# Stick-breaking attention: two-head score tiles in two PSUM banks, the second sigmoid in SBUF, units in a written order

## The chip, the cores and the metric

The kernel runs on one core of one Trainium2 chip. The metric is the device time of one execution in microseconds (us). Five engines work side by side, each through its own queue in order: TensorE (PE in the profile; PEld are its weight loads), VectorE (DVE), ScalarE (ACT), GpSimd (POOL) and SyncE (SP), which issues most DMAs.

## The reference

Two transformer layers on a sequence of 2048 tokens, width 1024. The first layer has six heads of stick-breaking attention, six of differential attention and four of memory attention; the second has sliding-window and memory attention. The change is in the six stick-breaking heads (head size 64), whose reference is, for a block of 128 queries:

```python
z = jnp.einsum('bqhd,bkhd->bhqk', qi, k, preferred_element_type=jnp.float32) * scale
strict = key_idx[None, :] < q_idx[:, None]
log_1mb = jnp.where(strict, jax.nn.log_sigmoid(-z), 0.0)
rc = jnp.flip(jnp.cumsum(jnp.flip(log_1mb, axis=-1), axis=-1), axis=-1)
after = rc - log_1mb
w = jnp.where(strict, jnp.exp(jax.nn.log_sigmoid(z) + after), 0.0)
return jnp.einsum('bhqk,bkhd->bqhd', w.astype(v.dtype), v)
```

So the weight of a key is sigmoid(z) times the product of sigmoid(-z) over all keys between it and the query. The kernel forms that product with a scan from the last key to the first.

## The kernel before

One launch runs stages one after the other: layer-1 projections, gates, stick-breaking, differential attention, the output product with layer norm, then layer 2. A scheduler that works with modelled times orders the instructions on each engine; where code goes through `PinnedCore`, the named engines keep the order in which the code is written (such instructions carry the helper's line, L55, in the profile, and L57 in the changed file).

Stick-breaking (`stick_breaking`) works on three pairs of heads (p), four blocks of 512 queries (t, from the last), four blocks of 128 queries in each (qi, from the last), and chunks of 512 keys (c, from the diagonal backwards). One (p, t, qi, c) is called a unit here; there are 120. A unit on the diagonal has 512, 384, 256 or 128 columns (qi = 3 to 0), every other 512. For each of a unit's two heads the steps are:

- scores: two matmuls (L572) into a PSUM bank z, and on the diagonal a third that adds the mask (L575);
- ScalarE: sigmoid(z/8) into an SBUF tile wb (L577), then sigmoid(-z/8) over z in PSUM (L578);
- VectorE: a scan (L581) of running products from PSUM into an SBUF row of products; its second operand is a column of zeros in SBUF; GpSimd sets each row's last element to 1 (L563);
- wb times that row (L585), four times in five on GpSimd and once on VectorE;
- `tblocks`: up to four TensorE transposes into a bank tp (L474), copied to SBUF as wT in turn by ScalarE (L121) and VectorE (L123);
- values (L591): per block of 128 keys one product for each head, into halves of the bank pv. Each stands in the trace as two records.

At the end of a block t VectorE multiplies pv by a gate (L595), and SyncE stores it. PSUM has four banks for z, three for tp, one for pv. None of the stage's instructions go through `PinnedCore`. When p = 2 and t = 1 are reached in the code, `filler` asks for the first weights of the next stage's background work: loads into rx, CASTs on ScalarE into wo (L871), subtractions on GpSimd (L872). The scheduler is free to put these earlier.

Of the kernel before, what the change touches and what calls it, by code (L numbers as in the profile page):

```python
# [7 lines left out]
F32 = mybir.dt.float32  # L8
# [3 lines left out]
AF = mybir.ActivationFunctionType  # L12
ALU = mybir.AluOpType
# [4 lines left out]
P = 128  # L18
NB = S // P
TC = 512  # L20
NT = S // TC
# [11 lines left out]
FT = 1  # L33
# [5 lines left out]
FILL = 0.95  # L39
PRODUCTS = ((), (0, 1), (), (2, 3))  # L40
# [24 lines left out]
class Net:  # L65
# [216 lines left out]
    def layer1_proj(self):  # L282
        nc, dr = self.nc, self.dr
# [82 lines left out]
        for k, _ in enumerate(gates):  # L366
            if k == 24 + GATES_A:
                self.sb_first = self.load_sb(0)
# [158 lines left out]
    def load_sb(self, p):  # L527

        qs = self.load_qstack(self.sbq[p], NT - 1)
# [8 lines left out]
        return ks, vp, qs  # L538

    def stick_breaking(self):  # L540
        nc = self.nc
        for p in range(3):
            ks, vp, qs = self.load_sb(p) if p else self.sb_first
            for t in range(NT - 1, -1, -1):
                if p == 2 and t == FT:
                    self.fill = self.filler()
                    for f in next(self.fill):
                        f()
                    self.dk, self.dq = {}, {}
                    self.load_dq(0, 0, 0)  # L550
                    for c in range(NT - 1):
                        self.load_dk(0, c)
                if t < NT - 1:
                    qs = self.load_qstack(self.sbq[p], t)
                sl = self.load_silu(self.silu[p], t)
                pv = self.psum("pv")
                for qi in range(3, -1, -1):
                    qb = 4 * t + qi
                    qcol = slice(qi * P, (qi + 1) * P)
                    n = (qb + 1) * P  # L560
                    pr = [self.t("row") for _ in range(2)]
                    for hh in range(2):
                        nc.gpsimd.memset(pr[hh][:, n - 1:n], 1.0)  # L563
                    for c in range(qb // 4, -1, -1):
                        lo, hi = c * 512, min(n, c * 512 + 512)
                        m = hi - lo
                        ws = []
                        for hh in range(2):
                            z = self.psum("z")
                            diag = hi == n  # L570
                            for k in range(2):
                                nc.tensor.matmul(z[:, :m], qs[:, hh, k, qcol], ks[hh][:, lo:hi], start=(k == 0),  # L572
                                                 stop=(k == 1 and not diag))
                            if diag:
                                nc.tensor.matmul(z[:, m - P:m], self.identb, self.mask[:, 2 * P + 1:3 * P + 1], start=False, stop=True)  # L575
# [12 lines left out]
                        for j in range(m // P):  # L588
                            blk = c * 4 + j
                            for hh in range(2):  # L590
                                nc.tensor.matmul(pv[64 * hh:64 * hh + 64, qcol], vp[:, blk, 64 * hh:64 * hh + 64],  # L591
                                                 wT[hh][:, j * P:(j + 1) * P],
                                                 start=(hi == n and j == 0), stop=(c == 0 and j == m // P - 1))
                mt = self.t("c2")
                nc.vector.tensor_mul(mt, pv, sl)  # L595
                self.dma(self.m1[p, :, t * TC:(t + 1) * TC], mt, nc.scalar if p == 2 and t == 0 else None)

# [765 lines left out]
    def run(self):  # L1363
        nc, dr, i = self.nc, self.dr, self.i
        with self.phase({"kv": 6, "qs": 2}, {}):
# [4 lines left out]
            with self.phase({"row": 5, "wb": 5, "wT": 5, "c2": 2, "sl": 2}, {"z": 4, "tp": 3, "pv": 1}, "right"):  # L1370
                self.stick_breaking()
# [95 lines left out]
```

## Time and profile before

| | |
|---|---|
| median of 3 runs | 2593.26 us (2591.59 to 2594.64) |
| profiled execution, its own time | 2590.89 us |
| its span, first to last instruction | 2589.1 us |
| mean granted TensorE clock | 0.983 of full speed |
| TensorE, VectorE, ScalarE, GpSimd busy in the span | 95%, 63%, 49%, 35% |
| stick-breaking stage in the span | about 720 to 1117 us |

The span is measured inside one execution; its own time also holds what lies around it. The stage's limits are read from the first score matmul at 720.63 us and the last multiplication by a gate, which begins at 1117.24 us.

### The profile page before, as it was taken

The numbers are of one execution on the slowest core, as the hardware profiler recorded it, in microseconds if no ns is written. First come the engines' busy times: TensorE is split into PE (matmuls) and PEld (weight loads), VectorE is DVE, ScalarE is ACT, GpSimd is POOL, SyncE is SP. The second block draws the span as 40 slices with busy tenths as digits, with TensorE's granted clock in tenths as the row PEclk, the third lists the DMA queues.
The fourth block names the chain that finished last, engine by engine and source line by source line (L and its number), as shares of the span: only waits on it lengthen the run. The fifth ranks groups of instructions, "written<-read, shape, count | busy, mean of one in ns | idle before, by whom it ended". The sixth has DMA issues, their size and how long they took to land. (4 is left out here: it accounts for less than half of the span.)

```text
span 2589.1 us, 42439 instructions
## 1 busy us (share of the span) xinstructions
PE 2450.0 (95%) x15564; PEld 1952.1 (75%) x15564; DVE 1626.6 (63%) x3744; ACT 1261.8 (49%) x2653; POOL 897.5 (35%) x752
## 2 busy tenths in 40 slices
PE   8999999999979999989888889899999999999998
PEld 7778998888857777757666667778788777777887
DVE  4833223531159999979899899795311776677455
ACT  4442222221147777747777677543211777776200
POOL 0401003750036655620110121364621655534333
PEclk9999999999989999989999999999999999999999
DMA  7643222331571422263454332463323555523541
GB/s 287 208 158 129 74 84 90 126 126 48 140 177 42 107 50 50 58 161 99 107 123 123 99 98 63 147 207 128 82 90 116 146 161 155 149 93 106 194 146 65
DMA packets 199247, 311.59 MB, mean 120 GB/s; under 512 B 17920, under 2 KB 97280, under 8 KB 198528
## 3 DMA queue, kind: packets, MB, share of 16 engines
q1 hardware_dynamic: 198464, 307.83, 40.2%
q8 instruction: 123, 2.02, 0.3%
q10 hardware_dynamic: 576, 1.05, 0.1%
q14 instruction: 84, 0.69, 0.1%
HBM read 204.74 MB, written 104.07 MB: 119 GB/s over the span
## 5 line engine op out<-in xcount | busy, mean ns | idle before, releaser
L55 PE MATMUL psmm<-big,w 128*128 128x512 f32 x1680 | 413.8, 394 | 0.0
L55 PEld LDWEIGHTS psmm<-big,w 128*128 128x128 f32 x1680 | 305.8, 189 | 57.6
L581 DVE TENSOR_TENSOR_SCAN row<-psz,row,zero 128x512 f32<-128x512 f32 (+5 forms) x240 | 258.6, 1108 | 34.1 <-ACT psz L578 33.8
L252 PE MATMUL psmm<-big,w 128*128 128x512 f32 x1200 | 275.2, 389 | 0.0
L585 POOL TENSOR_TENSOR wb<-wb,row 128x512 f32<-128x512 f32 (+3 forms) x192 | 219.3, 1152 | 133.0 <-DVE row L581 123.1
L252 PEld LDWEIGHTS psmm<-big,w 128*128 128x128 f32 x1200 | 225.0, 188 | 47.0 <-issue 0.2
L55 PE MATMUL psmm<-big,mp 128*128 128x512 f32 x1056 | 245.0, 392 | 1.4 <-POOL big L962 1.4
L55 ACT ACTIVATE row<-row,mn 128x2048 f32<-128x2048 f32 (+7 forms) x192 | 229.8, 1202 | 11.8 <-DVE mn L728 7.3
L55 PEld LDWEIGHTS psmm<-big,mp 128*128 128x128 f32 x1056 | 198.4, 189 | 43.0 <-POOL big L962 1.8
L722 DVE TENSOR_SCALAR_CACHE_REDUCE row<-psz 128x512 f32<-128x512 f32 (+1 forms) x324 | 200.5, 639 | 25.1 <-PE psz L55 24.5
L1181 DVE TENSOR_TENSOR c<-psmm,c 128x512 f32<-128x512 f32 x62 | 42.7, 691 | 240.3 <-ACT c L1180 240.2
L55 ACT COPY wT<-pstp 128x512 f32<-128x512 f32 (+3 forms) x240 | 121.0, 522 | 116.7 <-PE pstp L55 114.0
L591 PE MATMUL pspv<-wT,kv 128*64 128x128 f32 x1632 | 158.0, 287 | 17.2 <-ACT wT L121 17.2
L892 POOL TENSOR_TENSOR mp<-mp,mp 128x640 fp32r<-128x640 f32 x32 | 52.2, 1632 | 347.4 <-ACT mp L55 297.3
L577 ACT ACTIVATE wb<-psz 128x512 f32<-128x512 f32 (+3 forms) x240 | 129.8, 541 | 53.5 <-PE pstp L474 38.4
L591 PEld LDWEIGHTS pspv<-wT,kv 128*64 128x64 f32 x1632 | 106.7, 139 | 62.3 <-issue 20.7
L572 PE MATMUL psz<-kv,qs 128*128 128x512 f32 (+3 forms) x480 | 150.0, 406 | 2.1 <-DVE row L581 2.0
L55 PE MATMUL psmm<-wo,mp 128*128 128x512 f32 x480 | 148.0, 421 | 3.2 <-ACT mp L55 2.5
L764 DVE SCALAR_TENSOR_TENSOR row<-row,tiny,row 128x128 f32<-128x128 f32 (+7 forms) x144 | 149.9, 1090 | 0.4
L1180 ACT ACTIVATE c<-psmm 128x512 f32<-128x512 f32 x62 | 36.7, 596 | 211.7 <-PE psmm L252 203.8
L207 POOL TENSOR_TENSOR w<-w,w 128x1024 fp32r<-128x1024 f32 x20 | 48.6, 2432 | 257.5 <-ACT w L206 154.5
L55 PE MATMUL pstp<-ident,row 128*128 128x128 f32 x816 | 130.1, 280 | 6.6 <-ACT wT L55 5.6
(220 smaller groups left out, 5073.6 us busy)
## 6 DMA issues: line engine op xcount, KB each, us to landing
silu<-c SPq DMA_DIRECT2D x54, 256.0 KB, 2.3
sl<-silu SPq DMA_DIRECT2D x54, 256.0 KB, 3.2
qs<-sbq SPq DMA_DIRECT2D x48, 256.0 KB, 5.3
cs<-rope SPq DMA_DIRECT2D x24, 512.0 KB, 4.4
kc<-k SPq DMA_DIRECT2D x36, 320.0 KB, 5.0
w<-in_we_dram SPq DMA_DIRECT2D x20, 512.0 KB, 3.7
raw<-in_wo_dram SPq DMA_DIRECT2D x20, 512.0 KB, 3.9
rx<-in_x_dram SPq DMA_DIRECT2D x32, 256.0 KB, 2.8
```

What stands on the lines that cost most here:

```text
L55: return self.tc.keep_in_program_order(f(*a, **k))
L207: eng.tensor_sub(lo[:, sl], raw[:, sl], hi[:, sl].bitcast(F32))
L252: self.nc.tensor.matmul(ps, w[a][:, c, :], self.xpart(t, c, b), start=(c == k == 0), stop=(c == 7 and k == 2))
L572: nc.tensor.matmul(z[:, :m], qs[:, hh, k, qcol], ks[hh][:, lo:hi], start=(k == 0), stop=(k == 1 and not diag))
L577: nc.scalar.activation(w[:, :m], z[:, :m], AF.Sigmoid, scale=0.125)
L581: nc.vector.tensor_tensor_scan(prr[:, lo + s0 - 1:hi - 1][:, ::-1], z[:, s0:m][:, ::-1], self.zero.to_broadcast([P, m - s0]), prr[:, hi - ...
L585: eng.tensor_mul(w[:, :m], w[:, :m], prr[:, lo:hi])
L591: nc.tensor.matmul(pv[64 * hh:64 * hh + 64, qcol], vp[:, blk, 64 * hh:64 * hh + 64], wT[hh][:, j * P:(j + 1) * P], start=(hi == n and j == ...
L722: nc.vector.tensor_scalar(e[:, col + lo:col + lo + n0], z[:, :n0], -scale, before, ALU.mult, ALU.min, accum_out=acc)
L764: self.nc.vector.scalar_tensor_tensor(x[:, lo:hi], y[:, lo:hi], cf[hh][:, w:w + 1], x[:, lo:hi], ALU.mult, ALU.add)
L892: self.nc.gpsimd.tensor_sub(ml, m, mh.bitcast(F32))
L1181: nc.vector.tensor_mul(sg, ps, sg)
```

## The change

The stage is rewritten as functions for the parts of a unit, and a loop that calls them in a fixed order:

- A z tile has two banks and holds both heads; there are two such tiles. Each sigmoid is one instruction over both heads. sigmoid(-z/8) is done first and goes to a new SBUF tile `s` (three of them); sigmoid(z/8) follows.
- The scan reads its products from `s` in SBUF. Its zeros now lie in PSUM, in a bank of their own; tp has two banks instead of three.
- All multiplications of weights by products are on GpSimd. Copies of transposed weights follow the pattern ScalarE, ScalarE, VectorE.
- TensorE and ScalarE keep the written order: scores three units ahead, then the transposes and copies of the present unit, then the sigmoids three units ahead, and the value products of two units together every second time. VectorE, GpSimd and SyncE are still ordered by the scheduler.
- The queries of the next block are asked for when a block begins, and the keys and values of the next pair at t = 2.

```diff
+SB_AHEAD = 3
+SB_GROUP = 2
...
     def stick_breaking(self):
...
-                            w = self.t("wb")
-                            nc.scalar.activation(w[:, :m], z[:, :m], AF.Sigmoid, scale=0.125)
-                            nc.scalar.activation(z[:, :m], z[:, :m], AF.Sigmoid, scale=-0.125)
-                            s0 = 1 if lo == 0 else 0
-                            prr = pr[hh]
-                            nc.vector.tensor_tensor_scan(
-                                prr[:, lo + s0 - 1:hi - 1][:, ::-1], z[:, s0:m][:, ::-1], self.zero.to_broadcast([P, m - s0]),
-                                prr[:, hi - 1:hi], ALU.mult, ALU.add)
-                            eng = nc.gpsimd if self.turn("mul", "PPPPV") == "P" else nc.vector
-                            eng.tensor_mul(w[:, :m], w[:, :m], prr[:, lo:hi])
-                            ws.append(w)
-                        wT = [self.tblocks([w[:, j * P:(j + 1) * P] for j in range(m // P)]) for w in ws]
...
+        nc = self.nc
+        self.nc = pinned = PinnedCore(nc, self.tc, ("tensor", "scalar"))
...
+        def scores(u):
...
+            z = self.psum("z", [P, 2, 512])
+            for hh in range(2):
+                for k in range(2):
+                    self.nc.tensor.matmul(z[:, hh, :m], qs[p, t][:, hh, k, qi * P:(qi + 1) * P], kv[p][0][hh][:, lo:hi], start=(k == 0),
+                                          stop=(k == 1 and not diag))
...
+        def weights(u):
...
+            rest = self.t("s", F32, [P, 2, 512])
+            self.nc.scalar.activation(rest[:, :, :m], z[:, :, :m], AF.Sigmoid, scale=-0.125)
+            w = ws[u] = self.t("wb", F32, [P, 2, 512])
+            self.nc.scalar.activation(w[:, :, :m], z[:, :, :m], AF.Sigmoid, scale=0.125)
+            for hh in range(2):
+                prr = prs[p, t, qi][hh]
+                nc.vector.tensor_tensor_scan(
+                    prr[:, lo + s0 - 1:hi - 1][:, ::-1], rest[:, hh, s0:m][:, ::-1], zero.to_broadcast([P, m - s0]),
+                    prr[:, hi - 1:hi], ALU.mult, ALU.add)
+                nc.gpsimd.tensor_mul(w[:, hh, :m], w[:, hh, :m], prr[:, lo:hi])
+
+        def turn(u):
+            n, lo, hi = bounds(u)
+            w = ws.pop(u)
+            wTs[u] = [self.tblocks([w[:, hh, j:j + P] for j in range(0, hi - lo, P)], "AAV") for hh in range(2)]
...
+        zero = self.psum("zero")[:, :1]
+        nc.vector.memset(zero, 0.0)
+        for u in units[:SB_AHEAD]:
+            scores(u)
+            weights(u)
+        for k, u in enumerate(units):
+            if k + SB_AHEAD < len(units):
+                scores(units[k + SB_AHEAD])
+            turn(u)
+            if k + SB_AHEAD < len(units):
+                weights(units[k + SB_AHEAD])
+            while k - done >= SB_GROUP or k == len(units) - 1 and done <= k:
+                for v in units[done:done + SB_GROUP]:
+                    values(v)
+                done += SB_GROUP
...
-            with self.phase({"row": 5, "wb": 5, "wT": 5, "c2": 2, "sl": 2}, {"z": 4, "tp": 3, "pv": 1}, "right"):
+            with self.phase({"row": 4, "wb": 4, "s": 3, "wT": 7, "c2": 2, "sl": 2}, {"z": 2, "tp": 2, "pv": 1, "zero": 1}, "right"):
```

VectorE before, a place in the first block of queries (pair 0, t = 3). The scans (L581, printed as SCALAR_TENSOR_TENSOR) read psz; L123 copies transposed weights, L585 multiplies weights by products:

```order
L581 SCALAR_TENSOR_TENSOR row_6067<-psz_6145,row_6067,zero 128x512
L581 SCALAR_TENSOR_TENSOR row_6068<-psz_6153,row_6068,zero 128x512
L581 SCALAR_TENSOR_TENSOR row_6067<-psz_6183,row_6067,zero 128x511
L585 TENSOR_TENSOR wb_6186<-wb_6186,row_6067 128x512
L123 COPY wT_6135<-pstp_6130 128x512
L581 SCALAR_TENSOR_TENSOR row_6068<-psz_6191,row_6068,zero 128x511
L581 SCALAR_TENSOR_TENSOR row_6221<-psz_6225,row_6221,zero 128x256
L581 SCALAR_TENSOR_TENSOR row_6222<-psz_6234,row_6222,zero 128x256
L123 COPY wT_6173<-pstp_6168 128x512
```

The same place in the changed kernel, where the scan is L604 and the copy L125, and pszero is the bank of zeros:

```order
L604 SCALAR_TENSOR_TENSOR row_5990<-s_6086,row_5990,pszero_5909 128x512
L604 SCALAR_TENSOR_TENSOR row_5991<-s_6086,row_5991,pszero_5909 128x512
L604 SCALAR_TENSOR_TENSOR row_5990<-s_6111,row_5990,pszero_5909 128x511
L604 SCALAR_TENSOR_TENSOR row_5991<-s_6111,row_5991,pszero_5909 128x511
L125 COPY wT_6158<-pstp_6153 128x512
L604 SCALAR_TENSOR_TENSOR row_6135<-s_6160,row_6135,pszero_5909 128x256
L604 SCALAR_TENSOR_TENSOR row_6136<-s_6160,row_6136,pszero_5909 128x256
```

The multiplication has left VectorE, and for the same six scans one copy stands there instead of two. Each copy is that of a unit whose own scans lie at least two scans back.

ScalarE before, at the start of the stage: three tiles (of one head each) have their sigmoids, then come three CASTs of the next stage's weights (L871), the first copy and more sigmoids:

```order
L577 ACTIVATE wb_5994<-psz_5991 128x512
L578 ACTIVATE psz_5991<-psz_5991 128x512
L871 CAST wo_10140<-rx_10134 128x512
L871 CAST wo_10145<-rx_10136 128x512
L871 CAST wo_10150<-rx_10138 128x512
L121 COPY wT_5936<-pstp_5931 128x512
L577 ACTIVATE wb_6002<-psz_5999 128x512
L578 ACTIVATE psz_5999<-psz_5999 128x512
```

ScalarE in the changed kernel, from the second unit on, where the CASTs are L920 and the stage's own instructions L57:

```order
L57 ACTIVATE s_5942<-psz_5937 128x1024
L57 ACTIVATE wb_5944<-psz_5937 128x1024
L920 CAST wo_9768<-rx_9762 128x512
L920 CAST wo_9773<-rx_9764 128x512
L920 CAST wo_9778<-rx_9766 128x512
L57 ACTIVATE s_5955<-psz_5950 128x1024
L57 ACTIVATE wb_5957<-psz_5950 128x1024
L57 COPY wT_5973<-pstp_5968 128x512
L57 COPY wT_5980<-pstp_5975 128x512
L57 ACTIVATE s_5982<-psz_5963 128x1024
L57 ACTIVATE wb_5984<-psz_5963 128x1024
```

The three CASTs stay near the start; two units of two heads are ahead of them instead of five tiles of one head, and one instruction covers both heads. From then on the copies of unit k stand ahead of the sigmoids of unit k + 3.

## Rows read from the trace of the kernel before

**Rows 1.** Page, part 1: busy us (share of the span) and instructions.

```profile
PE 2450.0 (95%) x15564; PEld 1952.1 (75%) x15564; DVE 1626.6 (63%) x3744; ACT 1261.8 (49%) x2653; POOL 897.5 (35%) x752
```

**Rows 2.** Windows: length, busy of PE, PEld, DVE, ACT, POOL; clock, DMA share, GB/s.

```profile
759.80:1117.20 357.40, 357.05 (x2908) 258.06 (x2906) 334.79 (x402) 261.25 (x574) 217.56 (x275) 0.99 0.25 59
775.00:1100.00 325.00, 324.65 (x2645) 234.11 (x2646) 307.04 (x367) 238.88 (x523) 198.13 (x249) 1.00 0.26 61
```

**Rows 3.** Waits, 720 to 1120 us: us in total, times, longest.

```profile
ACT wb L577 <- PE pstp L474: 38.4, 37, 2.8
DVE row L581 <- ACT psz L578: 33.8, 26, 11.7
```

**Rows 4.** Timeline of ScalarE and VectorE near the start: start, us, instruction, [idle before].

```profile
739.43 1.66 ACT L871 CAST wo<-rx 128x512 fp32r<-128x512 f32 x3 [12.96 <-DMA m<-c]
741.96 0.59 ACT L578 ACTIVATE psz<-psz 128x512 f32<-128x512 f32 x1
742.59 5.64 DVE L581 TENSOR_TENSOR_SCAN row<-psz,row,zero 128x512 f32<-128x512 f32 x5 [11.72 <-ACT psz L578]
757.67 0.62 ACT L871 CAST wo<-rx 128x512 fp32r<-128x512 f32 x1 [6.68 <-DMA rx<-in_woute_dram]
759.80 1.28 DVE L581 TENSOR_TENSOR_SCAN row<-psz,row,zero 128x512 f32<-128x512 f32 x1 [6.75 <-ACT psz L578]
```

**Rows 5.** Windows: scans (DVE); multiplications (DVE, POOL); transposes, copies (PE, PEld, DVE, ACT).

```profile
759.80:1117.20 357.40, 245.70 (x229) 0.99 0.25 59
...
759.80:1117.20 357.40, 33.04 (x46) 209.34 (x184) 0.99 0.25 59
...
759.80:1117.20 357.40, 129.12 (x784) 86.34 (x782) 67.76 (x116) 60.80 (x116) 0.99 0.25 59
```

**Rows 6.** Groups by line and shape, 720 to 1120 us: busy, mean ns, idle before.

```profile
L585 POOL TENSOR_TENSOR wb<-wb,row 128x512 f32<-128x512 f32 x144 | 182.4, 1276 | 114.0 <-DVE row L581 106.1 <-PE pspv L591 4.4 <-PE pstp L474 3.0
L591 PE MATMUL pspv<-wT,kv 128*64 128x128 f32 x1632 | 158.0, 287 | 17.2 <-ACT wT L121 17.2
L581 DVE TENSOR_TENSOR_SCAN row<-psz,row,zero 128x512 f32<-128x512 f32 x90 | 112.7, 1271 | 27.7 <-ACT psz L578 27.6
L577 ACT ACTIVATE wb<-psz 128x512 f32<-128x512 f32 x168 | 101.7, 605 | 45.9 <-PE pstp L474 36.7 <-PE psz L572 7.3 <-PE psz L575 0.9
L123 DVE COPY wT<-pstp 128x512 f32<-128x512 f32 x84 | 56.3, 670 | 6.6 <-PE pstp L474 6.3
L121 ACT COPY wT<-pstp 128x512 f32<-128x512 f32 x84 | 49.6, 591 | 33.0 <-PE pstp L474 32.0
L585 DVE TENSOR_TENSOR wb<-wb,row 128x512 f32<-128x512 f32 x24 | 16.8, 701 | 0.3
```

**Rows 7.** Timeline: instructions of one kind back to back.

```profile
711.79 9.00 PE L252 MATMUL psmm<-big,w 128*128 128x512 f32 x39
899.34 3.62 DVE L581 TENSOR_TENSOR_SCAN row<-psz,row,zero 128x512 f32<-128x512 f32 x3
900.82 0.66 PE L474 MATMUL pstp<-ident,wb 128*128 128x128 f32 x4
1111.54 0.98 PE L474 MATMUL pstp<-ident,wb 128*128 128x128 f32 x7
1113.75 1.09 PE L591 MATMUL pspv<-wT,kv 128*64 128x128 f32 x16
```

**Rows 8.** Groups by shape, whole run: ScalarE instructions of 1024 columns.

```profile
L206 ACT CAST w<-w 128x1024 fp32r<-128x1024 f32 x20 | 21.0, 1049 | 28.9 <-PE psmm L252 9.2 <-DMA w<-in_we_dram 8.1 <-PE psmm L55 7.1
```

**Rows 9.** Timeline: multiplications of weights on GpSimd and VectorE.

```profile
905.22 1.27 POOL L585 TENSOR_TENSOR wb<-wb,row 128x512 f32<-128x512 f32 x1 [0.78 <-DVE row L581]
905.48 1.15 DVE L585 TENSOR_TENSOR wb<-wb,row 128x128 f32<-128x128 f32 x1
1114.83 0.29 DVE L585 TENSOR_TENSOR wb<-wb,row 128x128 f32<-128x128 f32 x1
```

More of the change, by code (lines that the diff above doesn't have):

```diff
@@ L537, in load_sb @@
         self.dma(vp, self.v1[:, :, p * P:(p + 1) * P].rearrange("b k f -> k b f"))
-        return ks, vp, qs
+        return ks, vp
     def stick_breaking(self):
         nc = self.nc
[L542 to L575, printed above, removed]
-                            w = self.t("wb")
-                            nc.scalar.activation(w[:, :m], z[:, :m], AF.Sigmoid, scale=0.125)
-                            nc.scalar.activation(z[:, :m], z[:, :m], AF.Sigmoid, scale=-0.125)
-                            s0 = 1 if lo == 0 else 0
-                            prr = pr[hh]
-                            nc.vector.tensor_tensor_scan(
-                                prr[:, lo + s0 - 1:hi - 1][:, ::-1], z[:, s0:m][:, ::-1], self.zero.to_broadcast([P, m - s0]),
-                                prr[:, hi - 1:hi], ALU.mult, ALU.add)
-                            eng = nc.gpsimd if self.turn("mul", "PPPPV") == "P" else nc.vector
-                            eng.tensor_mul(w[:, :m], w[:, :m], prr[:, lo:hi])
-                            ws.append(w)
-                        wT = [self.tblocks([w[:, j * P:(j + 1) * P] for j in range(m // P)]) for w in ws]
[L588 to L593, printed above, removed]
@@ new lines, in stick_breaking, with begin @@
+        self.nc = pinned = PinnedCore(nc, self.tc, ("tensor", "scalar"))
+        chunks = [(p, t) for p in range(3) for t in range(NT - 1, -1, -1)]
+        units = [(p, t, qi, c) for p, t in chunks for qi in range(3, -1, -1) for c in range(t, -1, -1)]
+        kv, qs, sls, prs, zs, ws, wTs, pvs = {0: self.sb_first[:2]}, {(0, NT - 1): self.sb_first[2]}, {}, {}, {}, {}, {}, {}
+        def begin(p, t):
+            sls[p, t] = self.load_silu(self.silu[p], t)
+            k = chunks.index((p, t)) + 1
+            if k < len(chunks):
+                qs[chunks[k]] = self.load_qstack(self.sbq[chunks[k][0]], chunks[k][1])
+            if t == NT - 2 and p < 2:
+                kv[p + 1] = self.load_sb(p + 1)
+            if p == 2 and t == FT:
+                self.fill = self.filler()
+                self.nc = nc
+                for f in next(self.fill):
+                    f()
+                self.nc = pinned
+                self.dk, self.dq = {}, {}
+                self.load_dq(0, 0, 0)
+                for c in range(NT - 1):
+                    self.load_dk(0, c)
@@ new lines, in bounds @@
+        def bounds(u):
+            p, t, qi, c = u
+            n = (4 * t + qi + 1) * P
+            return n, c * 512, min(n, c * 512 + 512)
+        def scores(u):
+            p, t, qi, c = u
+            n, lo, hi = bounds(u)
+            m, diag, s0 = hi - lo, hi == n, int(lo == 0)
+            if qi == 3 and c == t:
+                begin(p, t)
+            if c == t:
+                prs[p, t, qi] = [self.t("row", F32, [P, 2048]) for _ in range(2)]
+                for hh in range(2):
+                    nc.gpsimd.memset(prs[p, t, qi][hh][:, n - 1:n], 1.0)
+            z = self.psum("z", [P, 2, 512])
[3 more added lines that the diff above has]
+                                          stop=(k == 1 and not diag))
+                if diag:
+                    self.nc.tensor.matmul(z[:, hh, m - P:m], self.identb, self.mask[:, 2 * P + 1:3 * P + 1], start=False, stop=True)
+            zs[u] = z
@@ new lines, in turn, with values @@
+        def turn(u):
+            n, lo, hi = bounds(u)
+            w = ws.pop(u)
+            wTs[u] = [self.tblocks([w[:, hh, j:j + P] for j in range(0, hi - lo, P)], "AAV") for hh in range(2)]
+        def values(u):
+            p, t, qi, c = u
+            n, lo, hi = bounds(u)
+            if qi == 3 and c == t:
+                pvs[p, t] = self.psum("pv")
+            pv, wT, nj = pvs[p, t], wTs.pop(u), (hi - lo) // P
+            for j in range(nj):
+                for hh in range(2):
+                    self.nc.tensor.matmul(pv[64 * hh:64 * hh + 64, qi * P:(qi + 1) * P], kv[p][1][:, 4 * c + j, 64 * hh:64 * hh + 64],
+                                          wT[hh][:, j * P:(j + 1) * P], start=(hi == n and j == 0), stop=(c == 0 and j == nj - 1))
+            if qi == 0 and c == 0:
@@ L594, in stick_breaking @@
                 mt = self.t("c2")
-                nc.vector.tensor_mul(mt, pv, sl)
+                nc.vector.tensor_mul(mt, pvs.pop((p, t)), sls.pop((p, t)))
                 self.dma(self.m1[p, :, t * TC:(t + 1) * TC], mt, nc.scalar if p == 2 and t == 0 else None)
+        done = 0
+        zero = self.psum("zero")[:, :1]
[13 more added lines that the diff above has]
+                done += SB_GROUP
@@ L598, in differential @@
+        self.nc = nc
     def differential(self):
```

8 lines of the change are left out of this document (6 added, 2 removed).

## The prediction

> **What bounds the kernel now.** I began with the page's table of engines [rows 1]: TensorE is busy for 95% of the span and VectorE for 63%. The reader should not stop there, since the change touches one stage. The timeline puts that stage, stick-breaking, between 720 and 1117 us, so I asked for busy time by stretch [rows 2]. In its steady part, 775 to 1100 us, TensorE is busy 324.65 of 325 us, weight loads fill 234.11, VectorE 307.04 (94.5%), ScalarE 238.88, GpSimd 198.13. Two engines look full. TensorE is not: its matmuls overlap and their ends are modelled, so its busy time includes waits. The weight loads leave 28% of the stretch free. By the Trainium skill (Perfetto Trace Analysis, Identifying the Most-Contended Engine) matmul busy time is a poor measure for TensorE and the share of weight loads a good one. This trace agrees: read by the first, the stage could not become shorter without fewer matmuls; read by the second, 258.06 us of weight loads in the last 357.4 us leave room.
>
> The list of waits between 720 and 1120 us confirms VectorE [rows 3]: the scan waits for ScalarE's second sigmoid only 33.8 us in 26 times, and 11.7 of them are one event, while ScalarE waits 38.4 us for TensorE's transposes. That one event is in the timeline [rows 4]: ScalarE holds three CASTs of the next stage's weights, which wait for a DMA until 739.43, and VectorE starts again at 742.59. A fourth CAST ends at 758.3 after another DMA wait, and VectorE waits 6.75 us, until 759.80. From there to the end at 1117.2 VectorE is busy 334.79 of 357.4 us, 93.7% [rows 2].
>
> **The change, part by part.** A unit is a block of 128 queries against up to 512 keys, for two heads; there are 120.
>
> *The start.* ScalarE's order (quoted above) still has the three CASTs early, now behind two units instead of two and a half, and the fourth after unit 4. They wait for DMAs whose place in SyncE's queue has not moved, so I keep both stalls and compare from 759.80 on. Eleven scans are done by then before (229 of 240 fall in the later stretch, one of them across the line [rows 5]); I expect ten in the changed kernel.
>
> *VectorE.* All multiplications of weights by running products go to GpSimd: VectorE loses 46 of them, 33.0 us [rows 5]. Copies of transposed weights go from one in two to one in three, 120 to 80. VectorE's 116 copies after 759.80 take 67.8 us, 0.58 each, for 78 left of the new pattern: 38 x 0.58 = 22.2 us less. One more scan remains: 1.2 us. VectorE's work from 759.80 is 334.8 - 33.0 - 22.2 + 1.2 = 280.8 us.
>
> *The scan itself* reads its products from SBUF and its zeros from PSUM, instead of the reverse. No row has that form. The present one takes 1271 ns for 512 columns [rows 6], 3.62 us for three back to back [rows 7]. Other two-operand work has nearly the same price with a source in either memory (the SBUF multiplication takes 701 ns, the PSUM copy 670 ns [rows 6]), so I take no difference; the bounds are no change, and the wait of a rival below.
>
> *GpSimd* gets the 46 multiplications: 209.3 / 184 = 1.14 us each [rows 5], 209.3 + 52.3 = 262 us. It stays below VectorE.
>
> *ScalarE* copies 156 instead of 116 tiles: 60.8 / 116 = 0.52, so +21 us. Its sigmoids take both heads at once. No row reads two PSUM banks; the nearest is a CAST of 1024 columns in 1049 ns [rows 8], against 2 x 605 for two heads now [rows 6]: 0.16 saved for each of 230 merges, 37 us; the lower bound is no saving, since neighbours overlap. From 261.3 [rows 2] this makes 245 to 282 us; I take the middle, below VectorE.
>
> *TensorE* does the same matmuls. A score matmul follows the last after 9.00 / 39 = 0.23 us (39 products of the same size, back to back), a transpose after (0.98 - 0.66) / 3 = 0.11, a value record after (1.09 - 0.29) / 15 = 0.053 [rows 6, 7]. A full unit has 4, 8 and 16: 0.92 + 0.88 + 0.85 = 2.65 us. VectorE needs two scans at 1.2 and 2/3 of a copy: 2.8. The 816 transposes and 1632 value records are 102 full units, so TensorE needs about 102 x 2.65 = 270 us of it, with masks about 275, less five units: some 262.
>
> All four engines therefore need less than 282 us, and VectorE most. If it were 93.7% busy as now, the stage would end at 759.8 + 280.8 / 0.937 = 1059.5.
>
> *The fixed order* decides whether it is. Scores stand three units ahead, and unit k+3's sigmoids stand behind unit k's copies on ScalarE. So from the end of unit k's scan to the start of unit k+3's there lies: GpSimd's multiplication of the second head 1.28, its transposes 0.66, the copy 0.59, the merged sigmoid 1.04 [rows 6 to 8], and four hand-offs, which I estimate at 0.1 (a scan starts 0.04 us after its sigmoid [rows 4]): 4.0 us. The cover is VectorE's work on units k+1 and k+2, 2 x 2.8 = 5.6. On TensorE the products of two units stand as one block of 32 x 0.053 = 1.7 us ahead of every second unit's scores and transposes; it makes the transposes up to 0.9 late (1.7 + 2.65 - 0.85 = 3.5 between two units' transposes, against VectorE's 2.8, rounded up for the changes from one kind of matmul to another), and 4.9 is still covered. It is not where a unit is short. On the diagonal units have 512, 384, 256 or 128 columns; 128 cost VectorE about 0.9 us, so a pair with it covers 3.7, and short by 0.3 to 1.2. Two such gaps for each of the four 128-column rows of a head pair, smaller ones at 256 columns, and some 3 us at the last block (t = 0, four diagonal units in a row) come to about 7 us for a pair, 21 for three, an estimate; with 4 us to drain the last unit, 25. VectorE would be busy 280.8 of 306 us (92%), and the stage ends at 1066 instead of 1117.2: 51.4 us earlier.
>
> *Nothing takes it back.* The weight loads and key blocks of the next stage reuse buffers of this one and follow its end; its first order on each engine is the same, so it moves earlier as a whole.
>
> **Sum.** The profiled execution took 2590.9 us (span 2589.1), against a median of 2593.3. 2590.9 - 51.4 = 2539.5; I say 2540.
>
> **The rivals.** *The cover holds everywhere.* VectorE never waits after 759.8: 1041 and 4 us to drain, 72 us saved, 2519. Against it stand the short units.
>
> *TensorE's order becomes the bound.* If each block of products delays the next scan by its 0.9 us, some 57 blocks give back 51 us in full; if half of them do, 26, and the time is 2566. For it speaks that TensorE's 2.65 us is within 6% of VectorE's 2.8; against it the 1.6 us of cover over the bare 4.0.
>
> *Slower: the scan waits for GpSimd.* In the timeline VectorE's multiplication of 128 columns, both operands in SBUF, takes 1.15 us while GpSimd's 1.27 us multiplication runs, and 0.29 where GpSimd is idle [rows 9]. If the scan from SBUF waited in the same way, each of 230 scans would lie behind a multiplication of 1.14 us: +262 us, less the 51 gained, 2802. It decides from 51 / 230 = 0.22 us a scan. Against it: today's scan too has one streamed operand in SBUF (the zeros) and a first element from there, and stays at 1271 ns with GpSimd 61% busy. The Trainium skill (SBUF — State Buffer, Who interferes with whom) says the same in general: two SBUF inputs contend with GpSimd's reads, one does not. By that rule the changed scan is free; whether the element that carries the product counts as an input, no run here shows yet.
>
> *No difference.* All 57 blocks delay, or the next stage starts no earlier because its key blocks land when they do now: 2590. No row speaks for a fixed landing time.
>
> **How the numbers follow.** My case, 2527 to 2553, has 0.62; full cover 0.13; TensorE's order 0.14; no difference 0.04; slower 0.07 (4 for the scan that waits, 3 for an order that costs more than the whole gain). A measurement of this kernel tells about 0.2%, 5 us, from no change. Faster 0.89, same 0.04, slower 0.07. The range runs from 2512, full cover with a few microseconds from the first stalls, to 2568, TensorE's order at half price; it leaves out about 0.15.
>
> **What would show it.** Right: 240 multiplications on GpSimd, scans at 1.27 us, merged sigmoids near 1.04, two stalls before 760, VectorE 90 to 94% busy from there, the first scores of the next stage near 1067. Wrong: scans whose duration varies with GpSimd; sigmoids over two banks near 1.2 us, which brings ScalarE to VectorE's level; VectorE waiting for ScalarE again and again, with ScalarE waiting for TensorE's transposes, and weight loads well over 80% of the stage; or a stage as short as forecast and a later one that is longer.

## The result, and the profile after

The changed kernel took 2560.84 us (median of 4 runs, 2559.07 to 2566.42), against 2593.95 for the kernel before in the runs beside it (4 runs; the median of three was 2593.26). The ratio is 0.9877 [0.9859 to 0.9895]: 33 us faster. The forecast was 2540, 53 us faster, with a range from 2512 to 2568. The sign and the range held; two fifths of the gain did not come.

The profiled execution of the changed kernel took 2562.38 us, its span is 2560.5, its mean clock 0.981. Its table of engines, against [rows 1]:

```profile
PE 2394.9 (94%) x15564; PEld 1942.7 (76%) x15564; DVE 1572.5 (61%) x3657; ACT 1253.9 (49%) x2453; POOL 942.9 (37%) x800
```

VectorE has 87 instructions fewer, GpSimd 48 more, ScalarE 200 fewer, and TensorE the same. The stage comes first again: the timeline of ScalarE and VectorE at its start (start, us, instruction, idle before), against [rows 4]:

```profile
739.54 1.66 ACT L920 CAST wo<-rx 128x512 fp32r<-128x512 f32 x3 [14.23 <-DMA m<-c]
742.15 2.45 DVE L604 TENSOR_TENSOR_SCAN row<-s,row,pszero 128x512 f32<-128x512 f32 x2 [14.69 <-ACT s L57]
...
755.16 0.62 ACT L920 CAST wo<-rx 128x512 fp32r<-128x512 f32 x1 [6.32 <-DMA rx<-in_woute_dram]
757.22 2.45 DVE L604 TENSOR_TENSOR_SCAN row<-s,row,pszero 128x512 f32<-128x512 f32 x2 [5.79 <-ACT s L57]
```

Both stalls are there as forecast, the second 2.6 us earlier. At 757.22 ten scans are done and 230 are left. Windows of the stage (columns as in [rows 2]): from the eleventh scan, in the steady part, and from the forecast's own mark. The first and the last reach to VectorE's first instruction of the next stage at 1083.06:

```profile
757.20:1083.10 325.90, 305.38 (x2937) 248.48 (x2936) 285.72 (x321) 255.75 (x387) 256.11 (x322) 1.00 0.28 65
775.00:1065.00 290.00, 273.14 (x2628) 222.82 (x2624) 258.56 (x287) 231.54 (x348) 232.57 (x289) 1.00 0.29 68
759.80:1083.10 323.30, 302.78 (x2928) 246.58 (x2928) 283.27 (x319) 254.85 (x386) 254.98 (x322) 1.00 0.27 64
```

From 759.80 on VectorE works 283.3 us, where 280.8 were forecast. But it takes 323.3 us for them, not 306: it is busy 87.6% of the time, where 92% was forecast and 93.7% stood before [rows 2]. It idles 40.0 us against 25. Those 15 us and the 2.5 of work make the 17 us between the forecast's 1066 and 1083.06. (By the forecast's own mark, the last multiplication by a gate, the stage ends at 1082.45, 16.4 us late.) What VectorE waits for is in the list of waits, 757.2 to 1083 us (total, times, longest; the longest of the fourth row, 5.8, is the start stall):

```profile
ACT wT L57 <- PE pstp L57: 64.0, 69, 2.3
POOL wb L607 <- DVE row L604: 45.4, 46, 2.8
PEld pstp L57 <- POOL wb L607: 25.1, 31, 2.1
DVE row L604 <- ACT s L57: 22.5, 28, 5.8
DVE wT L125 <- PE pstp L57: 20.4, 20, 2.2
PE pstp L57 <- DVE wT L125: 13.8, 25, 1.5
```

Without the start stall the scans wait 16.7 us for their sigmoids, a little less than the 21 that the prediction gave to the short units. By VectorE's timeline 13.1 of these stand at scans where one of the two units before has 256 or 128 columns. Beside it stands a wait that it did not have: 20 of VectorE's copies wait 20.4 us for transposes. TensorE's transposes in their turn wait 13.8 us for those copies, since pstp has two banks. No engine is full, and each waits for another.

The prices, from the groups by shape, 715 to 1120 us (busy, mean ns, idle before), against [rows 6]:

```profile
L607 POOL TENSOR_TENSOR wb<-wb,row 128x512 f32<-128x512 f32 x168 | 211.3, 1283 | 64.8 <-DVE row L604 46.7 <-ACT wT L57 10.8 <-PE pstp L57 4.0
L604 DVE TENSOR_TENSOR_SCAN row<-s,row,pszero 128x512 f32<-128x512 f32 x90 | 109.6, 1264 | 30.4 <-ACT s L57 29.4 <-POOL row L584 0.6
L57 ACT ACTIVATE s<-psz 128x1024 f32<-128x1024 f32 x84 | 87.8, 1045 | 0.5 <-PE psz L57 0.5
L125 DVE COPY wT<-pstp 128x512 f32<-128x512 f32 x56 | 37.6, 671 | 7.6 <-PE pstp L57 7.4
```

The scan from SBUF costs 1264 ns (1271 before), the sigmoid over two banks 1045 (forecast 1.04 us), the multiplication 1283. All durations were right; the waiting was not.

### The profile page after: what moved, and what is told of

Same layout as the page of the kernel before. It is cut to its first block, busy times and chain, and to the rows that moved or that the text cites. A ratio compares the mean times of both kernels' runs of the same rounds, so it can differ in the third digit from the quotient of the medians.

```text
span 2560.5 us, 42280 instructions
## 1 busy us (share of the span) xinstructions
PE 2394.9 (94%) x15564; PEld 1942.7 (76%) x15564; DVE 1572.5 (61%) x3657; ACT 1253.9 (49%) x2453; POOL 942.9 (37%) x800
## 5 line engine op out<-in xcount | busy, mean ns | idle before, releaser
L57 PE MATMUL psmm<-big,w 128*128 128x512 f32 x1680 | 414.5, 394 | 0.0
L57 PEld LDWEIGHTS psmm<-big,w 128*128 128x128 f32 x1680 | 306.1, 189 | 57.8
L57 ACT COPY wT<-pstp 128x512 f32<-128x512 f32 (+3 forms) x400 | 203.2, 525 | 190.9 <-PE pstp L57 186.6
L607 POOL TENSOR_TENSOR wb<-wb,row 128x512 f32<-128x512 f32 (+3 forms) x240 | 262.5, 1119 | 69.0 <-DVE row L604 49.1
L604 DVE TENSOR_TENSOR_SCAN row<-s,row,pszero 128x512 f32<-128x512 f32 (+5 forms) x240 | 252.2, 1102 | 38.8 <-ACT s L57 37.2
L57 PE MATMUL psmm<-big,mp 128*128 128x512 f32 x1056 | 244.9, 392 | 1.4 <-POOL big L1011 1.4
L57 ACT ACTIVATE row<-row,mn 128x2048 f32<-128x2048 f32 (+7 forms) x192 | 229.7, 1201 | 12.0 <-DVE mn L777 8.4
L57 PEld LDWEIGHTS psmm<-big,mp 128*128 128x128 f32 x1056 | 198.4, 189 | 42.9 <-POOL big L1011 1.8
L57 PE MATMUL psz<-kv,qs 128*128 128x512 f32 (+3 forms) x480 | 134.9, 399 | 17.7 <-ACT wb L57 17.4
L57 PE MATMUL psmm<-wo,mp 128*128 128x512 f32 x480 | 148.1, 421 | 3.5 <-ACT mp L57 2.8
L57 PE MATMUL pstp<-ident,wb 128*128 128x128 f32 x816 | 117.3, 278 | 24.9 <-DVE wT L125 13.8
L57 PE MATMUL pstp<-ident,row 128*128 128x128 f32 x816 | 131.0, 282 | 7.0 <-ACT wT L57 6.2
L57 PEld LDWEIGHTS pstp<-ident,wb 128*128 128x128 f32 x816 | 92.9, 142 | 45.1 <-POOL wb L607 25.1
L1187 ACT ACTIVATE e<-e,tiny 128x256 f32<-128x256 f32 (+1 forms) x192 | 94.6, 494 | 60.4 <-DVE e L1185 59.8
```

The costliest lines, as they stand in the source:

```text
L57: return self.tc.keep_in_program_order(f(*a, **k))
L604: nc.vector.tensor_tensor_scan(prr[:, lo + s0 - 1:hi - 1][:, ::-1], rest[:, hh, s0:m][:, ::-1], zero.to_broadcast([P, m - s0]), prr[:, hi ...
L607: nc.gpsimd.tensor_mul(w[:, hh, :m], w[:, hh, :m], prr[:, lo:hi])
L1187: nc.scalar.activation(e[:, hh, ns:], e[:, hh, ns:], AF.Exp, bias=nmx[:, hh:hh + 1], scale=-1.0, accum_out=s[:, hh:hh + 1])
```

## The experiments

Two theories stood against each other for the missing 20 us. **A:** the loop of four engines is longer than its cover, so that sigmoids come late; then the number of units ahead decides. **B:** TensorE's written order makes transposes late, above all its blocks of value products, and VectorE's copies wait behind them. A third question was which part of the change brings the gain at all. All edits are against the changed kernel; ratios are against the kernel before, run on the same chip. The kernel before ran beside each group of kernels, at medians of 2591.8 to 2594.0 us, so differences of absolute times between groups are uncertain by some 2 us. "Stretch" is the time from the eleventh scan to VectorE's first instruction of the next stage: 325.9 us in the changed kernel, 367.5 in the one before (6.75 of them its second start stall, which there comes behind the eleventh scan).

### The zeros in SBUF

```diff
-        zero = self.psum("zero")[:, :1]
-        nc.vector.memset(zero, 0.0)
+        zero = self.zero
```

> The changed kernel with one edit: the scan's zeros come from the SBUF column that the kernel before used, not from PSUM, so both streamed operands of the scan lie in SBUF. Theory (two SBUF operands make VectorE wait for GpSimd's multiplications, one does not): scans no longer stay at 1.26 us; many of 230 wait for a multiplication of up to 1.28 us, mean 1.5 us or more, stage longer by 60 to 260 us. Rival (a column that is read again and again is no stream, so the bank of zeros buys nothing): scans 1.26 to 1.28 us, time within 5 us of the changed kernel's 2561.

Measured: 2680.06 us, 1.0341 [1.0324 to 1.0359]; the stretch is 440.8 us. Groups by shape, 720 to 1300 us, of this kernel:

```profile
L607 POOL TENSOR_TENSOR wb<-wb,row 128x512 f32<-128x512 f32 x168 | 330.7, 1995 | 40.0 <-DVE row L604 32.4 <-ACT wT L57 3.9 <-PE pstp L57 2.3
L604 DVE TENSOR_TENSOR_SCAN row<-s,row,zero 128x512 f32<-128x512 f32 x90 | 152.3, 1737 | 14.6 <-ACT s L57 14.2 <-POOL row L584 0.3
L604 DVE TENSOR_TENSOR_SCAN row<-s,row,zero 128x511 f32<-128x511 f32 x78 | 147.2, 1926 | 0.5 <-ACT s L57 0.4
...
L604 DVE TENSOR_TENSOR_SCAN row<-s,row,zero 128x128 f32<-128x128 f32 x18 | 22.2, 1272 | 0.7 <-ACT s L57 0.7
```

One column of zeros, read again and again, decides. VectorE is now busy 418.80 of the 440.8 us. With both streams of the scan in SBUF, scan and GpSimd's multiplication take 1737 to 1926 and 1995 ns instead of 1264 and 1283; a scan of 128 columns takes 1272 instead of 462. It is GpSimd that makes the scan slow, not the second SBUF operand by itself: in this same kernel the five scans of 512 columns that meet no multiplication take 1276 to 1290 ns, and the 50 that have one beside them for over nine tenths of their time take 2218 at the median. Two of them from VectorE's timeline, at 892 and at 897 us; GpSimd's multiplications of that place begin at 893.35:

```profile
891.90 1.28 DVE L604 TENSOR_TENSOR_SCAN row<-s,row,zero 128x512 f32<-128x512 f32 x1
...
896.43 2.22 DVE L604 TENSOR_TENSOR_SCAN row<-s,row,zero 128x512 f32<-128x512 f32 x1
```

The slower rival of the prediction is a real mechanism, at less than half of its price of 262 us, and the bank of zeros in PSUM keeps it away: it is worth 119 us (2680.06 - 2560.84), which is nearly all in the stretch (440.8 - 325.9 = 115). The Trainium skill (SBUF — State Buffer, Who interferes with whom) says that a VectorE instruction with two SBUF inputs contends with a GpSimd instruction that reads SBUF, and that one with at most one SBUF input, outside the two-port modes that the page names, does not. These two runs agree, and they settle what was open: the element that carries the product does not count as an input, a column broadcast along the row does.

### One unit's products at a time

```diff
-SB_GROUP = 2
+SB_GROUP = 1
```

> The changed kernel with the value products after every unit instead of two units' together, so that the block ahead of the next transposes on TensorE is 0.85 us instead of 1.7. Theory A (the idle 40 us of VectorE come from the loop scan, multiplication, transposes, copy, sigmoid where a unit is short; TensorE's blocks are covered): within 5 us of 2561. Theory B (TensorE's order is what makes transposes late): VectorE's waits for transposes, 20 us now, halve, and the time falls by 5 to 15 us. Rival of both (TensorE's own work is the bound): 60 more changes between kinds of matmul at 0.1 to 0.2 us make it 6 to 12 us slower.

Measured: 2562.09 us, 0.9892 [0.9877 to 0.9906]; stretch 325.7 us. No difference. VectorE's copies hardly wait any more (5.1 us instead of 20.4), but in its place the scans wait 35.8 us for their sigmoids, 34 times; without the start stall these are 30.2, against 16.7. B in its narrow form, the blocks of two units, is wrong: without them the other wait takes over the whole time.

### Copies on ScalarE alone

```diff
-            wTs[u] = [self.tblocks([w[:, hh, j:j + P] for j in range(0, hi - lo, P)], "AAV") for hh in range(2)]
+            wTs[u] = [self.tblocks([w[:, hh, j:j + P] for j in range(0, hi - lo, P)], "A") for hh in range(2)]
```

> The changed kernel with all copies of transposed weights on ScalarE. VectorE loses 46 us of work and all 20 us of its waits for transposes, ScalarE gains 78 copies of 0.52, 41 us, and comes to 297 of 323. If VectorE bounds the stage (theory A): the time falls by 15 to 35 us. If TensorE's order does (theory B): within 8 us of 2561, and VectorE waits for ScalarE's sigmoids instead. If ScalarE becomes the bound: slower by up to 20 us.

Measured: 2546.18 us, 0.9833 [0.9817 to 0.9849], 15 us faster than the changed kernel. The stretch in the windows view and the waits in it (both of this kernel):

```profile
755.70:1069.20 313.50, 304.96 (x2932) 251.19 (x2932) 247.42 (x242) 284.93 (x465) 256.37 (x325) 0.98 0.29 68
```

```profile
DVE row L604 <- ACT s L57: 55.0, 56, 7.2
POOL wb L607 <- ACT wT L57: 24.1, 25, 2.0
ACT wT L57 <- PE pstp L57: 23.8, 35, 2.0
```

VectorE lost 38 us of work, ScalarE took over 29 and became the fullest engine (284.93 of 313.50, 91%), and the stretch is 12 us shorter. So VectorE's copies were worth taking away, but for 38 us of work one gets 12: ScalarE now sends the sigmoids late (55.0 us, of which 7.2 are the start stall). The gain lies just under the least that A gave it (15 us), and the wait is the one that B named.

### No written order

```diff
-        self.nc = pinned = PinnedCore(nc, self.tc, ("tensor", "scalar"))
+        self.nc = pinned = PinnedCore(nc, self.tc, ())
```

> The changed kernel with the written order taken away: the same tiles, engines and look-ahead, but the scheduler orders TensorE and ScalarE as it did before the change. It parts the gain of the moved work from that of the order. Theory A: the work alone brings most of it, 2555 to 2575. Theory B: the written order costs something, so this is faster than 2561, by 5 to 15 us. Rival (the order is what brings the gain): 2580 or more.

Measured: 2596.8 us, 1.0023 [1.0012 to 1.0033]; the stretch is 373.5 us, of which 5.35 are the second start stall, since here the eleventh scan comes before it, at 747.80. The waits in it:

```profile
POOL wb L607 <- ACT wb L601: 72.8, 48, 4.6
DVE row L604 <- ACT s L599: 40.5, 35, 5.0
DVE wT L125 <- PE pstp L477: 37.4, 31, 5.3
```

All work is where the changed kernel has it, VectorE works 288.8 us in the stretch, and still nothing is gained over the kernel before. Both theories of this expectation are wrong; its rival came. Moving work off VectorE does not by itself make the stage shorter. The written order without the moved work was not run. VectorE's own order is the scheduler's in every kernel here and may change with each edit.

### Order on TensorE alone, order on ScalarE alone

```diff
-        self.nc = pinned = PinnedCore(nc, self.tc, ("tensor", "scalar"))
+        self.nc = pinned = PinnedCore(nc, self.tc, ("tensor",))
```

> The changed kernel with the written order on TensorE alone; the scheduler orders ScalarE. Without any written order the time was 2597 and GpSimd waited 66 us for the second sigmoid, which the scheduler had put behind a copy. If ScalarE's order is what pays: 2585 to 2600 here, and GpSimd waits for that sigmoid again. If TensorE's order pays: 2558 to 2570.

The other kernel has `("scalar",)` in that place.

> The changed kernel with the written order on ScalarE alone; the scheduler orders TensorE. If ScalarE's order is what pays: 2558 to 2572, and GpSimd no longer waits for the second sigmoid. If TensorE's order pays: 2585 to 2600. If each needs the other: both this and the run with TensorE alone at 2575 or more.

Measured: TensorE's order alone 2572.3 us, 0.9934 [0.9913 to 0.9954], stretch 341.2; ScalarE's alone 2597.41 us, 1.0024 [1.001 to 1.0038], stretch 360.1. The leading waits of the second, in its stretch:

```profile
ACT wT L57 <- PE pstp L477: 93.7, 116, 2.5
POOL wb L607 <- DVE row L604: 51.6, 47, 4.6
DVE row L604 <- ACT s L57: 40.8, 40, 4.9
```

With the scheduler's order on TensorE, ScalarE's fixed copies wait 93.7 us for transposes (64.0 in the changed kernel), and the sigmoids behind them come late. Against no order (2596.8), TensorE's order alone brings 24.5 us, ScalarE's alone nothing, and ScalarE's on top of TensorE's another 11.5 (by medians; by the ratios 23 and 15).

### Units ahead: two, and four

```diff
-SB_AHEAD = 3
+SB_AHEAD = 2
```

> The changed kernel with scores and sigmoids two units ahead instead of three. Theory A: the loop of 4.0 to 4.9 us then has one unit, 2.8 us, as cover, 1.2 to 2.1 us are missing in every two units, and the stage grows by 60 to 120 us. Theory B: 0 to 20 us, since the blocks on TensorE are the same.

For four ahead, one more tile `s` had to be paid with one wT:

```diff
-SB_AHEAD = 3
+SB_AHEAD = 4
...
-            with self.phase({"row": 4, "wb": 4, "s": 3, "wT": 7, "c2": 2, "sl": 2}, {"z": 2, "tp": 2, "pv": 1, "zero": 1}, "right"):
+            with self.phase({"row": 4, "wb": 4, "s": 4, "wT": 6, "c2": 2, "sl": 2}, {"z": 2, "tp": 2, "pv": 1, "zero": 1}, "right"):
```

> The changed kernel with scores and sigmoids four units ahead instead of three, a fourth tile s, and six wT tiles instead of seven (for space in SBUF). Theory A (the loop from one scan round to the scan three units later is not covered where units are short): with another unit as cover VectorE's waits for sigmoids, 17 us of the 40 idle, mostly go, and the time falls by 8 to 17 us. Theory B (TensorE's order makes transposes late): within 5 us of 2561.

Measured: two ahead 2596.5 us, 1.0008 [0.9999 to 1.0018], stretch 355.0; four ahead 2561.55 us, 0.9877 [0.9856 to 0.9898], stretch 328.8. The waits of VectorE and GpSimd with two ahead, from 757 to 1112 us (this takes in the second start stall of 8.2 us, which here ends at 764.41, and leaves out the last 7 us of the stretch):

```profile
POOL wb L607 <- DVE row L604: 72.6, 49, 3.5
...
DVE wT L125 <- PE pstp L57: 44.8, 35, 3.6
DVE row L604 <- ACT s L57: 28.5, 25, 8.2
```

Two ahead costs 29 us in the stretch, less than A's 60 to 120 and more than B's 20 at most. So the loop is one that the cover must pay for, but VectorE feels it at its copies more than at its sigmoids: in the stretch itself the copies wait 42.9 us (20.4 in the changed kernel), the scans 20.3 (16.7). Four ahead gives nothing, which A had at 8 to 17 us: the scans' wait falls to 12.0 us (18 times), the copies' rises to 26.4 (27 times). Three units is enough for the scans, and depth doesn't help the copies. With four ahead wT is one tile smaller, so that this run doesn't show the depth quite by itself.

### Half of the value products

This kernel leaves out the value products of the inner key blocks of a unit (at most two of four are done), so it does less than the reference asks for.

```diff
-            for j in range(nj):
+            for j in sorted({0, nj - 1}):
```

> The changed kernel with only the first and the last block of 128 keys of each chunk multiplied by the values, two of four (it leaves out that part of the value products): TensorE has some 36 us less work and its block ahead of the transposes is 0.85 us, with no more changes of kind. If TensorE's work or order binds (theory B): the time falls by 12 to 36 us. If the loop through the other engines binds (theory A): by 0 to 6 us.

Measured: 2546.69 us, 0.9816 [0.9794 to 0.9838]. The stretch in the windows view:

```profile
759.90:1068.30 308.40, 270.60 (x2233) 210.25 (x2232) 283.43 (x320) 255.31 (x388) 255.12 (x323) 0.99 0.29 69
```

With some 700 records of TensorE fewer, VectorE does the same work at 92% of the time, the forecast's share. Its copies wait 12.3 us instead of 20.4, and its scans 10.0 for sigmoids instead of 16.7 (both without the start stall). So TensorE's amount of work counts, though how its products are grouped does not (above): B in its wide form, TensorE too slow to keep transposes and scores ready, has part of the loss.

### The CASTs in the written order too

```diff
                 self.fill = self.filler()
-                self.nc = nc
                 for f in next(self.fill):
                     f()
-                self.nc = pinned
```

> The changed kernel with the next stage's five CASTs kept in ScalarE's written order too, so that they stand where the code has them (p = 2, t = 1) and not at the stage's start. VectorE's two waits there, 14.7 and 5.8 us, and 2 us behind the fifth CAST, go if ScalarE's queue is their cause: 15 to 22 us faster. Rival: the start is held by the DMA queue in another way (keys or queries land late), and less than 8 us comes of it.

Measured: 2548.5 us, 0.9828 [0.9809 to 0.9846], 12 us faster than the changed kernel, where 15 to 22 were expected. The eleventh scan begins at 737.30 instead of 757.22, the stretch from there takes 330.9 us, and VectorE's next stage begins at 1068.25 instead of 1083.06. The 20 us of start stalls can be had, and 15 of them arrive at the end of the stage. The other 5 are lost where the CASTs now stand. The timeline of ScalarE and VectorE there:

```profile
1021.13 1.70 ACT L57 CAST wo<-rx 128x512 fp32r<-128x512 f32 x3
1027.74 0.62 ACT L57 CAST wo<-rx 128x512 fp32r<-128x512 f32 x1 [4.90 <-DMA rx<-in_woute_dram]
1029.93 0.62 ACT L57 CAST wo<-rx 128x512 fp32r<-128x512 f32 x1 [1.57 <-DMA rx<-in_woute_dram]
...
1032.54 1.28 DVE L602 TENSOR_TENSOR_SCAN row<-s,row,pszero 128x512 f32<-128x512 f32 x1 [9.05 <-ACT s L57]
```

The fourth and fifth CAST again hold ScalarE for DMAs, which SyncE issues only at 1024.99 and 1027.4, and VectorE waits 9.05 us for a sigmoid behind them; the copies wait 16.6 us instead of 20.4. CASTs behind the whole stage were not tried. The prediction was right to keep the stalls for the kernel as it was.

### Both together, and multiplications back on VectorE

The edits of the kernels with late CASTs and with copies on ScalarE together:

> Two edits of earlier runs together: all copies on ScalarE and the next stage's CASTs late. Alone they brought about 15 and 13 us. If their gains are apart (one at the start, one in the steady part): 2530 to 2537. If VectorE and TensorE waiting for each other at the copies was the matter in both: 2540 or more.

And on top of them one multiplication in five on VectorE:

```diff
-                nc.gpsimd.tensor_mul(w[:, hh, :m], w[:, hh, :m], prr[:, lo:hi])
+                (nc.gpsimd if self.turn("mul", "PPPPV") == "P" else nc.vector).tensor_mul(w[:, hh, :m], w[:, hh, :m], prr[:, lo:hi])
```

> The same two edits, and every fifth multiplication back on VectorE, which has some 66 us idle in that stage. If the loop through GpSimd's multiplication of 1.28 us (0.70 on VectorE) now binds: 3 to 10 us faster than without. If VectorE's multiplication, with two operands in SBUF, waits for GpSimd's and delays scans: 3 to 12 us slower.

Measured: 2531.91 us, 0.9779 [0.9757 to 0.98], and 2532.15 us, 0.9776 [0.9756 to 0.9795]. The two gains add: 14.7 and 12.3 make 27.0, and 28.9 were measured. The second step changes nothing, where 3 to 10 us faster or 3 to 12 slower were expected, though it gives VectorE 27 us more to do (274.71 in its stretch of 315.9 us against 247.35) and takes 39 from GpSimd (223.80 against 262.91). In this kernel, then, taking the multiplications off VectorE is worth nothing. The stretch of the first in the windows view:

```profile
736.70:1054.80 318.10, 304.24 (x2943) 251.05 (x2944) 247.35 (x242) 287.20 (x469) 262.91 (x329) 0.99 0.35 82
```

2531.9 us is 1.1% under the changed kernel and 2.2% under the one before, and the best version of this study.

## Why the prediction was right, and what it mis-sized

**Right.** The scan's price, the merged sigmoid, the multiplications, both start stalls, ScalarE's 254.9 us (245 to 282 forecast, the middle 263) and, to 1%, VectorE's work. The rival in which the scan waits for GpSimd did not come, for the reason given, and the kernel with zeros in SBUF shows it where that reason is removed.

**The term that failed** is the idle time in "VectorE would be busy 280.8 of 306 us (92%)": 40 us instead of 25. Its 21 us for scans that wait at short units were about right in size and place (16.7 measured, 13.1 of them behind short units). What it lacked is the second wait, 20.4 us at VectorE's copies. The prediction priced a copy at 0.58 us of work, saved 38 of them, and put the remaining ones nowhere in VectorE's queue; in the kernel before, with three banks for tp, the 84 copies of 512 columns had waited 6.3 us for transposes [rows 6]. But VectorE takes its instructions in order: a copy that stands ahead of its transposes holds back the scans behind it, and a copy that stands behind two scans holds a bank that TensorE needs. The timeline of TensorE, VectorE and ScalarE in the changed kernel shows both, one after the other:

```profile
921.20 2.45 DVE L604 TENSOR_TENSOR_SCAN row<-s,row,pszero 128x512 f32<-128x512 f32 x2 [1.12 <-ACT s L57]
...
922.21 1.04 PE L57 MATMUL pstp<-ident,wb 128*128 128x128 f32 x8
...
923.57 0.67 DVE L125 COPY wT<-pstp 128x512 f32<-128x512 f32 x1
...
924.38 0.63 PE L57 MATMUL pstp<-ident,wb 128*128 128x128 f32 x4 [0.59 <-DVE wT L125]
...
924.94 1.97 PE L57 MATMUL pspv<-wT,kv 128*64 128x128 f32 x32
925.05 0.42 DVE L125 COPY wT<-pstp 128x256 f32<-128x256 f32 x1 [0.81 <-PE pstp L57]
...
926.84 1.20 PE L57 MATMUL psz<-kv,qs 128*128 128x512 f32 x4
...
929.48 1.03 ACT L57 ACTIVATE s<-psz 128x1024 f32<-128x1024 f32 x1
929.67 1.03 PE L57 MATMUL pstp<-ident,wb 128*128 128x128 f32 x8
...
930.31 0.69 DVE L125 COPY wT<-pstp 128x512 f32<-128x512 f32 x1 [1.74 <-PE pstp L57]
...
930.92 2.44 DVE L604 TENSOR_TENSOR_SCAN row<-s,row,pszero 128x512 f32<-128x512 f32 x2
```

The transposes of 922.21 end at 923.25; the copy follows only at 923.57, when two scans are done, and the transposes at 924.38, whose multiplications ended at 921.41, have waited 0.59 for its bank. VectorE's next copy waits 0.81 us for those, the one at 930.31 waits 1.74 for transposes that stand behind the block of products of 924.94 and another unit's scores and transposes; from 924.38 to there TensorE's records leave no gap. The last lines also show why a cure of one wait alone is worth little: the scans of 930.92 need the sigmoid that ends at 930.51, so without that copy VectorE would have gone on 0.4 us earlier, not 1.7. That is what one unit's products at a time and four units ahead measured: one wait fell, the other rose, the time stayed. Whether a third bank for tp would shorten the waits at the copies was not tried; the bank of zeros took its place.

**The work itself was a little too low,** 280.8 against 283.3, or 285.7 from 757.2 on, where the 230 scans that the forecast counted are left. The three groups of [rows 5] add up to 346.5 us, more than VectorE's 334.79: records of neighbours overlap, so an instruction taken out saves less than its duration. The prediction took out whole durations.

**How the gain comes about** was argued from the wrong end. The sum began with work taken from VectorE and let the busy share stand or fall with the order. The kernel without a written order has that work and no gain; TensorE's order alone brings 24.5 us. So the gain needs the order. How much of it the order would bring with the old share of work is not shown; the multiplications, given back to VectorE in the fastest kernel, cost nothing, while its copies, taken off, were worth 12 us of the stretch.

**TensorE as the bound,** the rival at 2566, had named the right engine: 2560.84 lies nearer to it than to 2540. But its mechanism, blocks of products that delay each scan by 0.9 us, is not what sets the time, since the kernel with single units' products takes as long. What is right of it: less work on TensorE shortens the stretch by 17 us. Of the signs of being wrong that the prediction named, one came in part: ScalarE waits 64.0 us for transposes and VectorE 16.7 for ScalarE, though weight loads fill only 76%.

**"Nothing takes it back"** failed by a few microseconds. VectorE's next stage begins 35.5 us earlier (1118.53 and 1083.06), the spans differ by 28.6. The first scores with the next keys, before and after, in the timeline of TensorE:

```profile
1122.24 0.59 PE L55 MATMUL psz<-kd,qa 128*128 128x512 f32 x1 [2.58 <-DMA kd<-dfk]
```

```profile
1089.65 0.77 PE L57 MATMUL psz<-kd,qa 128*128 128x512 f32 x1 [5.68 <-DMA kd<-dfk]
```

They come 32.6 us earlier, so 3 are lost in a longer wait for the keys: SyncE issues these loads 35.4 us earlier (1079.14 and 1114.52), but the four land after a median of 7.5 us instead of 5.0. That is not the price of being early: in the twelve other kernels this wait is 4.1 to 6.8 us, 4.96 in the one without a written order, whose stage ends later than that of before. The other 4 us lie in the 1471 us that follow (1467 before). In the profiled executions of all fourteen kernels this part takes 1466.4 to 1474.6 us, so 4 us is within its scatter, and the medians of the runs differ by 33.1. Why the keys take longer to land is open.

What stays open in the stage is the last of the waiting. In the fastest kernel ScalarE is busy 287.2 of 318.1 us and the scans wait 52.7 us for sigmoids (55 times, 9.0 of it once, behind the late CASTs). The Trainium skill (Perfetto Trace Analysis, Identifying the Most-Contended Engine) has one optimize the engine with the highest occupancy first. That engine is VectorE, at 88% of the changed kernel's stretch, and taking copies off it did pay: 12 us. That 38 us of work gave no more than these, while less work on TensorE gave 17, points to a ring of engines, 76% (weight loads) to 88% full, rather than a single one, as what sets the pace. Lighter ScalarE at an unchanged order was not tried.

## What to carry to other kernels

In a loop over engines that work in order, price an instruction by what it waits for and what waits behind it, not by its duration alone: 49 us of VectorE's work less (337.5 in the stretch before, 288.8 without a written order) gave nothing without the right order, and 78 short copies cost 20 us of waiting. When no engine is full, curing one wait moves the time to the next one, so judge an edit by the length of the stage and not by the wait that it removes. Work of a later stage that waits for a DMA holds up an in-order queue wherever it stands: moved from the start of the stage to its last fifth, five CASTs gained 12 us, since they saved 20 at the start and cost 9 at the new place.

## What was not expected of the hardware

A single broadcast column of zeros in SBUF made the scan and GpSimd's multiplication slow each other: 1264 to 1737 or 1926 ns and 1283 to 1995 ns at 512 columns, 462 to 1272 for a scan of 128, so that a scan of 128 columns then takes as long as an undisturbed one of 512. One activation over two PSUM banks takes 1045 ns where two over one bank take 605 each. And the mean granted clock of TensorE over the stretch was 0.90 in the kernel with zeros in SBUF, whose TensorE was busy 345.93 of 440.8 us, against 1.00 in the changed kernel with 305.38 of 325.9. With the two levels of 2.4 and 1.2 GHz, 0.90 is about a fifth of the stretch at the lower one.
